# Moving two small SBUF tiles ahead of the split input, so that input and weight blocks lie 256 bytes apart modulo 512

## The chip, the cores and the metric

The kernel runs on one core of one Trainium2 chip. The metric is the device time of one execution in microseconds (us), given as the median of the timed runs. An engine's row in the profile carries a short name: PE is the tensor engine's matmuls, PEld its loads of the stationary operand (LDWEIGHTS), DVE the vector engine, ACT the scalar engine, POOL and SP the other two. SBUF is the on-chip memory of 128 partitions; an offset in bytes below is always the offset within a partition.

## The reference, cut to what matters

Two layers of a decoder trunk on 256 tokens of 1024 channels, all in float32:

```python
for l in range(DEPTH):                      # 2
    h = _mixer(x, ...)                      # x @ w_in, then three branches:
                                            #   gated linear attention, retention, dilated window attention
                                            #   per-channel sigmoid gates, branch projections, merged @ w_out
    x = _layer_norm(ALPHA * x + h, ...)
    f = (silu(x @ w_gate) * (x @ w_up)) @ w_down
    x = _layer_norm(ALPHA * x + f, ...)
```

Nearly all arithmetic is products of the 256 tokens with weights that are used once.

## The kernel before

**Exact float32 products from float32r parts.** Every operand of a product with weights is split into two parts of type float32r: a rounded part (hi) and the rest (lo). A product then takes three matmuls: hi by hi, hi by lo and lo by hi. The layer's input is held split and transposed in the tiles `xh` (hi) and `xl` (lo), 8192 bytes each per partition (8 k-tiles of 256 tokens). The weights stream from HBM in 342 units of 128x1024 float32 into six `stage` buffers; ACT rounds a unit into one block of the pool `R` and DVE subtracts to make its lo part in another (`make_hi`, `make_lo`, recorded under line 118). `R` has 24 blocks of 4096 bytes, named `r` in the profile; the pools `F4` (7 blocks of 4160 bytes) and `F2` (10 of 2048), both named `f`, hold everything else.

**Two kinds of product.** Both are recorded under line 130, and a row names the output first, then the stationary and the moving operand among its inputs without telling which is which; the width does:

- `a_pair` computes [128 columns, 256 tokens]. The weights, 128 columns of an `r` block, are the stationary operand; 256 tokens of `xh` or `xl` are the moving one. Rows: `pm<-xh,r` and `pm<-xl,r`, 128x256. Used for the queries and keys of the dilated attention, for the merge gates, and for all but 512 channels of the SwiGLU.
- `b_group` computes [128 tokens, 512 columns]. 128 tokens of `xh` or `xl` are stationary and 512 columns of an `r` block move. Rows: `pm<-r,xh` and `pm<-r,xl`, 128x512. For the dilated groups' values the 128 tokens are every second one of 256 (`dl` = 2), so that the stationary operand spans 1024 bytes instead of 512.

Where the other operand is itself an activation that was split into `R` blocks, both operands are `r`: the branch projections (`pm<-r,r`, 128x256) and the SwiGLU's down projection (`px<-r,r`, 128x512). The gate of the linear attention multiplies `xh` and `xl` with the small tiles `gah` and `gal` (16 columns stationary, 64 bytes for each k-tile, 256 tokens moving; rows `px<-xh,gah` and so on).

**Order of the work.** The program's order on every engine is fixed when it is written, by a rough clock of costs that decides when side work (attention, norms, the next unit's split) is put between the products. In each layer the stages follow one another: dilated attention's projections, the other branches' projections, merge gates with branch projections, output projection and norm, SwiGLU in pairs of 128 columns (gate and up for one pair are 96 matmuls of 256 columns, then 24 of 512 for a pair's down projection), norm.

**Where tiles lie.** A pool hands out SBUF in the order in which tiles are first allocated, each rounded up to 32 bytes. Between the first `r` block and `xh` lie 24 x 4096 + 7 x 4160 + 10 x 2048 = 147904 bytes, which is 448 modulo 512; `xl` follows 8192 bytes later. So a slice of `xh` or `xl` that starts at a multiple of 512 bytes in its tile (those of lines 377 to 381 do; the odd tokens lie 4 bytes on) stands 64 bytes *behind* a slice of an `r` block, modulo 512, and two slices of `r` blocks stand 0 apart. After `xl` come the `stage` buffers, the constants, `pcol`, `edec` (32 bytes), `xres`, `gah`, `gal`, `hcol` (256 bytes) and the rest. By their sizes `gah` starts 352 bytes past `xh` modulo 512, `gal` too, and each k-tile of 16 columns in them 64 bytes past the one before.

Of the kernel before, what the change touches and what calls it, by code (L numbers as in the profile page):

```python
# [17 lines left out]
L = 2  # L18
# [4 lines left out]
ALPHA = (2 * L) ** 0.25  # L23
# [31 lines left out]
def trunk(ctx: ExitStack, tc: tile.TileContext, wst, xt_in, x_in, cst, tri, pcol, wga, wa2, lnp, out):  # L55
# [5 lines left out]
    def T(shape, tag, bufs=1, dt=F32):  # L61
        return sb.tile(shape, dt, tag=tag, name=tag, bufs=bufs)

    # ---- a rough clock in ns for each engine and tile: side work goes to the tensor engine when its operands
    # should be there, so that the products with the weights needn't wait behind it ----
    clk = {"P": 0.0, "A": 0.0, "V": 0.0, "G": 0.0, "D": 0.0}
# [7 lines left out]
    def when(log, ap, e):  # L74
        """When the last access in this log to any of the columns is over, as seen by engine e."""
        name, a, b = span(ap)
        return max([t + (e != "P" and OWN if by == e else HOP) for x, y, t, by in log.get(name, ()) if x < b and a < y], default=0.0)
# [44 lines left out]
    A = Timed(nc.scalar, "A", 0.833, 110)  # L122
# [17 lines left out]
    def settle(*aps, margin=MARGIN):  # L140
        """For a side generator: go on when these tiles should be there."""
        while any(when(written, a, "P") + margin > clk["P"] for a in aps):
            yield

# [1 line left out]
    class Blocks:  # L146
# [3 lines left out]
        def get(self, n=1):  # L150
            """For a side generator: the next n free blocks."""
            while len(self.free) < n:
                yield
            return [self.free.pop(0) for _ in range(n)]

        def main(self, n=1):
            """For the main stream."""
            left = 3000
            while len(self.free) < n:
                tick()  # L160
                left -= 1
                assert left, "blocks"
            return [self.free.pop(0) for _ in range(n)]
# [4 lines left out]
    R = Blocks(sb, NR, 1024, "r", F32R)  # L168
    F4 = Blocks(sb, N4, 1040, "f4")
    F2 = Blocks(sb, N2, 512, "f2")  # L170
    PM = Blocks(psp, 3, 512, "pm")
    PS = Blocks(psp, 5, 512, "px")

# [1 line left out]
    state = {"dma": 0, "made": 0, "whole": 0, "calm": False, "touched": 0, "freed": 0, "cap": NR // 2}  # L175
    staged, parts = {}, {}
    total = L * UNITS

    def halves(u):
        """The first unit goes by halves, for an early start."""  # L180
        return (slice(0, 512), slice(512, 1024)) if u == 0 else (slice(0, 1024),)
# [61 lines left out]

# [1 line left out]
    side = []  # L245
# [4 lines left out]
    def tick():  # L250
        for g in list(side):
            try:
                next(g)
            except StopIteration:
                side.remove(g)
        # the next unit: its first part when the engine is free for it, the second when the first should be there
        need = state["touched"] + 2
        late = clk["P"] + (CALM if state["calm"] else BACKLOG)
        if state["whole"] < state["made"]:
            hi = parts[state["whole"]][0]  # L260
            if state["whole"] < need or max(clk["V"], when(written, hi, "V")) < late:
                make_lo()
        if state["made"] < min(total, state["touched"] + AHEAD, state["whole"] + 2) and can_make():
            u = state["made"]
            there = u in staged and when(written, staged[u], "A") < clk["P"] + READY
            if u < need or there and min(clk["A"], clk["V"] - SWITCH) < late:
                make_hi()
# [14 lines left out]

# [1 line left out]
    XH = T([128, KT, S], "xh", 1, F32R)  # L284
    XL = T([128, KT, S], "xl", 1, F32R)
    xts = [F2.main()[0] for _ in range(4)]

    # the input comes in five pieces of k-tiles: 0, 1, 2-3, 4-5, 6-7
    PIECES = ((0, 1), (1, 2), (2, 4), (4, 6), (6, 8))
# [13 lines left out]

    # products of zeros while the first loads are under way bring the tensor engine to its full clock
    zero = F2.main()[0]
# [15 lines left out]
    PC = T([128, L, 32], "pcol")  # L321
    # the turning tables fill 32 partitions of their columns; the gate's second matrix and its bias lie beside them
    WA2 = C[32:49, COLS["dilc"][0]:COLS["dils"][1]].rearrange("p (l c) -> p l c", l=L)
    edec = T([128, 8], "edec")
    scr = {g: dram.tile([S, 520], F32, tag=f"scr{g}", name=f"scr{g}") for g in (1, 2)}
    xres = T([128, 2, D], "xres")
    GH = T([128, L, KT * 16], "gah", 1, F32R)
    GL = T([128, L, KT * 16], "gal", 1, F32R)
    hcol = T([128, L, 32], "hcol")
    TRI = T([128, 256], "tri", 1, F32R)  # L330

    def start_rest():
        """What the first products don't need."""
        dma(nc.scalar, C[0:32, 0:512], cst[0:32, 0:512], 32)
# [30 lines left out]
    half = T([128, 4], "half")  # L365
    V.memset(half, -0.5)
    one = T([128, 1], "one")
# [14 lines left out]

# [1 line left out]
    def tokens(v, tt, dl):  # L384
        """128 tokens: the tt-th half, or with dl = 2 those of remainder tt by 2."""
        return v[:, tt * 128:tt * 128 + 128] if dl == 1 else v.rearrange("p (i c) -> p c i", c=2)[:, tt, :]
# [11 lines left out]
    def b_group(units, lh, ll, tt, ps, dl=1, last=False):  # L398
        """ps [128 tokens, 512] from units of [2 k-tiles, 512 columns], a step for each unit."""
        n = len(units)  # L400
        for i, u in enumerate(units):
            b_unit(u, i, n, lh, ll, tt, ps, dl)
            if last:
                free(u)
            if i < n - 1:
                tick()

    def a_pair(units, rh, rl, ps):
        """ps [128 columns, 2, 256 tokens] from units of [4 k-tiles, 256 columns]."""
        n = len(units)  # L410
# [21 lines left out]

# [1 line left out]
    def ln_first(tt, c, ps, st):  # L434
# [36 lines left out]

# [1 line left out]
    def dil_rot(g, ps, dst):  # L473
        """Two heads' channels [128, 2, 256 tokens] into dst, their first 32 turned; dilated groups have even tokens first."""
        dl = 2 if g else 1
# [15 lines left out]
    def dil_group(l, g, dblk, m, den, outs):  # L491
        """Scores, softmax numerators and their products with v; outs gets [128 tokens, 512] for each tile."""
        qb, kb = dblk[g, 0], dblk[g, 1]
# [117 lines left out]

# [1 line left out]
    def gla_gates(l, E):  # L613
# [147 lines left out]

# [1 line left out]
    def ret_all(l, pss, vb, sg):  # L763
# [102 lines left out]
    def head_out(l, key, o, col):  # L866
        """A branch's [tokens, heads] transposed, times its norm's gain when col is given, and split."""
        OH, OL = OT[l, key] = yield from R.get(2)
# [22 lines left out]

# [1 line left out]
    for l in range(L):  # L893
# [3 lines left out]

        # the projections for the branches: a step by tokens has two tiles, one by channels two pairs of heads
        douts = {}
# [26 lines left out]

        # the first two have their units in turns: either tile of tokens, or piece of the first input, gives them work
        us = take(8)
# [61 lines left out]

        # merge gates and branch projections, by pairs of 128 columns
        state["cap"] = (NR - 10) // 2
# [39 lines left out]

        # output projection, then the first norm
        state["cap"] = (NR - 4) // 2
# [16 lines left out]

        # SwiGLU: the first 512 channels by tokens, the others by channels
        state["cap"] = (NR - 5) // 2
# [91 lines left out]
        for tt in range(2):  # L1145
            # of the last tile, the first half of the columns ends before the second begins
            st = T([128, 2, 6], "lnst", 2)
# [60 lines left out]
def _sums(np):  # L1208
    """Within each chunk of 64, a sixteenth of the sum up to a token and of the sum after it."""
    i = np.arange(128)  # L1210
    r, q = i[:, None], i[None, :]
    same = (r // 64) == (q // 64)
    return np.concatenate([np.where(same & (r <= q), 1 / 16, 0.0), np.where(same & (r > q), 1 / 16, 0.0)], 1).astype(np.float32)


def _stream(np, w_in, w_branch, w_out, w_gate, w_up, w_down):
    """All weights in the order of use, as units of [128, 1024]."""
    w = np.empty((L * UNITS, 128, 1024), np.float32)
# [100 lines left out]
```

## Time and profile before

| | |
|---|---|
| median of 3 timed runs | 1068.72 us (1066.67 to 1068.91) |
| the profiled execution's span, first to last instruction | 1066.5 us |
| PE busy | 1049.8 us (98%), 7122 matmuls |
| PEld busy | 956.9 us (90%) |
| DVE busy | 706.6 us (66%) |
| ACT busy | 491.8 us (46%) |
| DMA | 192.25 MB, mean 180 GB/s |

The page gives no other time of the profiled execution than its span; the lowest timed run lies 0.2 us above it, the median 2.2 us. PE's busy time runs from a matmul's start to its modelled end, so neighbouring matmuls overlap, and neither the busy time nor the mean duration of one says how fast they follow each other. That is read from the start times: the distance between two starts, divided by the number of matmuls that started in between. It is called the pace below.

### The profile page before, as it was taken

The page shows a single profiled execution, that of the slowest core. Times are in us where ns is not written, and L with a number is a line of the kernel's source. Part 1 is how long each engine was busy: PE and PEld are TensorE (multiplying, and loading weights), DVE is VectorE, ACT ScalarE, POOL GpSimd, SP SyncE. Part 2 cuts the span into 40 slices and gives each one's busy share as a digit, 9 for nine tenths or more (in the row PEclk, how much of TensorE's full clock was granted, in tenths as well). Part 3 has the DMA queues.
Part 4 walks back from the last instruction along what each step waited for, and adds up shares of the span by engine and source line. Part 5 has one row for each costly group of instructions (what it writes and reads, how often), then busy time and mean ns, then how long its engine had stood idle before and what let it go on. Part 6 is the DMA issues. An engine that isn't in the chain of part 4 may idle for free.

```text
span 1066.5 us, 17475 instructions
## 1 busy us (share of the span) xinstructions
PE 1049.8 (98%) x7122; PEld 956.9 (90%) x7122; DVE 706.6 (66%) x1065; ACT 491.8 (46%) x734; POOL 17.9 (2%) x24
## 2 busy tenths in 40 slices
PE   9999999999999999999999998999999999999997
PEld 7998977799998899999889998877999988999996
DVE  6798755767658756554688777476676686556454
ACT  6475554444445444343364554553443445444330
POOL 0000000000000000000000000000000000000000
PEclk9999999999999999999999999999999999999999
DMA  8786633426656574555376355343375666655521
GB/s 325 248 267 194 197 109 111 158 80 225 190 172 223 168 287 164 194 191 200 121 268 220 124 173 183 92 136 122 118 220 185 186 209 232 223 197 167 194 94 40
DMA packets 55667, 192.25 MB, mean 180 GB/s; under 512 B 6258, under 2 KB 7410, under 8 KB 55587
## 3 DMA queue, kind: packets, MB, share of 16 engines
q1 hardware_dynamic: 50400, 180.38, 51.4%
q10 hardware_dynamic: 5186, 10.76, 3.0%
q8 instruction: 56, 0.92, 0.3%
q14 instruction: 25, 0.20, 0.1%
HBM read 187.93 MB, written 3.18 MB: 179 GB/s over the span
## 4 chain that ended last, share of the span: by engine, by line
PE 90%; DVE 4%; DMA 3%; ACT 1%; issue 1%; SPq 0%; ACTq 0%; DVEq 0%
PE pm L130 70%; PE px L130 18%; DVE f L118 2%; PE px L134 2%; DMA scr<-f 2%; DVE r L118 2%; ACT f L118 1%; DMA stage<-in_wst_dram 0%; DMA f<-scr 0%; ACT r L118 0%; DVE xres L118 0%; SPq L138 0%; ACTq L138 0%; DVE lnst L118 0%; DVEq L1314 0%
## 5 line engine op out<-in xcount | busy, mean ns | idle before, releaser
L130 PE MATMUL pm<-xh,r 128*128 128x256 f32 x2688 | 478.2, 280 | 0.0
L118 DVE SCALAR_TENSOR_TENSOR r<-stage,r 128x1024 fp32r<-128x1024 f32 (+1 forms) x341 | 401.7, 1213 | 59.4 <-ACT r L118 57.1
L130 PEld LDWEIGHTS pm<-xh,r 128*128 128x128 f32 x2688 | 413.1, 189 | 1.1
L118 ACT ACTIVATE r<-stage 128x1024 fp32r<-128x1024 f32 (+1 forms) x328 | 332.8, 1051 | 91.8 <-issue 31.3
L130 PE MATMUL pm<-xl,r 128*128 128x256 f32 x1344 | 374.9, 279 | 0.0
L130 PEld LDWEIGHTS pm<-xl,r 128*128 128x128 f32 x1344 | 252.4, 188 | 0.9
L130 PE MATMUL pm<-r,xh 128*128 128x512 f32 x672 | 218.4, 406 | 0.8 <-ACT r L118 0.8
L130 PEld LDWEIGHTS pm<-r,xh 128*128 128x128 f32 x672 | 124.8, 192 | 29.3 <-issue 3.0
L130 PE MATMUL pm<-r,xl 128*128 128x512 f32 x336 | 133.6, 398 | 0.0
L118 ACT ACTIVATE f<-pm 128x512 f32<-128x512 f32 x72 | 50.8, 707 | 156.6 <-PE pm L130 106.1
L130 PE MATMUL px<-r,r 128*128 128x512 f32 x528 | 122.6, 389 | 0.0
L130 PEld LDWEIGHTS px<-r,r 128*128 128x128 f32 x528 | 97.9, 188 | 19.3
L130 PE MATMUL pm<-r,r 128*128 128x256 f32 (+1 forms) x768 | 115.1, 310 | 0.0
L130 PEld LDWEIGHTS pm<-r,r 128*128 128x128 f32 x768 | 105.2, 191 | 7.3
L118 DVE SCALAR_TENSOR_TENSOR f<-f,pm 128x512 f32<-128x512 f32 x52 | 35.6, 685 | 106.6 <-ACT f L118 89.9
L130 PEld LDWEIGHTS pm<-r,xl 128*128 128x128 f32 x336 | 64.6, 192 | 14.3
L130 PE MATMUL px<-f,f 128*128 128x128 f32 (+4 forms) x368 | 60.4, 304 | 6.3 <-DVE f L118 6.3
L130 PEld LDWEIGHTS px<-f,f 128*128 128x128 f32 (+2 forms) x368 | 48.7, 185 | 16.7 <-issue 8.5
L118 ACT ACTIVATE r<-f 128x512 fp32r<-128x512 f32 x28 | 17.7, 632 | 98.9 <-DVE f L118 98.9
L118 ACT ACTIVATE f<-pm,hcol 128x256 f32<-128x256 f32 x48 | 20.1, 471 | 58.1 <-PE pm L130 58.1
L118 ACT ACTIVATE f<-px 128x512 f32<-128x512 f32 (+2 forms) x52 | 25.0, 507 | 42.6 <-PE px L130 29.4
L118 DVE TENSOR_TENSOR f<-f,pm 128x512 f32<-128x512 f32 x22 | 15.1, 687 | 41.0 <-PE pm L130 40.8
(102 smaller groups left out, 498.6 us busy)
## 6 DMA issues: line engine op xcount, KB each, us to landing
stage<-in_wst_dram SPq DMA_DIRECT2D x339, 512.0 KB, 4.5
f<-in_lnp_dram ACTq DMA_DIRECT2D x8, 512.0 KB, 6.3
scr<-f ACTq DMA_DIRECT2D x8, 260.0 KB, 4.8
f<-scr ACTq DMA_DIRECT2D x4, 520.0 KB, 3.6
xres<-in_x_dram ACTq DMA_DIRECT2D x4, 256.0 KB, 4.0
out_dram<-xres SPq DMA_DIRECT2D x4, 256.0 KB, 2.0
f<-in_xt_dram SPq DMA_DIRECT2D x3, 256.0 KB, 9.1
cst<-in_cst_dram ACTq DMA_DIRECT2D x4, 192.0 KB, 3.8
```

The lines of the kernel that those rows point to most:

```text
L118: return f(*a, **k)
L130: return nc.tensor.matmul(out, lhsT, rhs, **k)
L134: return nc.tensor.transpose(out, in_, ident)
```

## The change

`hcol` and `edec` are allocated ahead of `xh`, with an unused tile of 32 bytes (`gap`) behind them: 256 + 32 + 32 = 320 bytes. The two later allocations go. Comments and documentation strings are emptied too. No instruction is added, removed or moved: the order of all instructions on all engines is the same.

```diff
+    hcol = T([128, L, 32], "hcol")
+    edec = T([128, 8], "edec")
+    T([128, 8], "gap")
     XH = T([128, KT, S], "xh", 1, F32R)
     XL = T([128, KT, S], "xl", 1, F32R)
     xts = [F2.main()[0] for _ in range(4)]
...
     WA2 = C[32:49, COLS["dilc"][0]:COLS["dils"][1]].rearrange("p (l c) -> p l c", l=L)
-    edec = T([128, 8], "edec")
     scr = {g: dram.tile([S, 520], F32, tag=f"scr{g}", name=f"scr{g}") for g in (1, 2)}
     xres = T([128, 2, D], "xres")
     GH = T([128, L, KT * 16], "gah", 1, F32R)
     GL = T([128, L, KT * 16], "gal", 1, F32R)
-    hcol = T([128, L, 32], "hcol")
     TRI = T([128, 256], "tri", 1, F32R)
```

So the distance from the first `r` block to `xh` becomes 147904 + 320 = 148224 bytes, 256 modulo 512. The `stage` buffers and the constants move by the same 320 bytes, `xres`, `gah` and `gal` by 288, what follows by 32. The pools `R`, `F4` and `F2` stay where they are.

## Rows read from the trace of the kernel before

**Rows 1.** The page's first part: busy us, share of the span, instructions.

```profile
span 1066.5 us, 17475 instructions
PE 1049.8 (98%) x7122; PEld 956.9 (90%) x7122; DVE 706.6 (66%) x1065; ACT 491.8 (46%) x734; POOL 17.9 (2%) x24
```

**Rows 2.** Windows: us, busy and count by engine, granted clock, DMA share, GB/s.

```profile
450.00:500.00 50.00, 50.00 (x360) 47.19 (x360) 26.64 (x27) 20.51 (x25) 0.00 (x0) 1.00 0.57 190
...
650.00:700.00 50.00, 46.83 (x273) 39.79 (x272) 27.86 (x50) 25.35 (x47) 1.05 (x2) 0.97 0.41 125
```

**Rows 3.** The chain that ended last: start us, us, what ran.

```profile
77.44 3.45 DVE r L118 x3
...
393.50 11.31 PE pm L130 x96
404.80 5.44 PE px L130 x24
```

**Rows 4.** Groups of PE instructions, shapes apart: count, busy us, mean ns, idle.

```profile
L130 PE MATMUL pm<-xh,r 128*128 128x256 f32 x2688 | 478.2, 280 | 0.0
L130 PE MATMUL pm<-xl,r 128*128 128x256 f32 x1344 | 374.9, 279 | 0.0
L130 PE MATMUL pm<-r,xh 128*128 128x512 f32 x672 | 218.4, 406 | 0.8 <-ACT r L118 0.8
L130 PE MATMUL pm<-r,xl 128*128 128x512 f32 x336 | 133.6, 398 | 0.0
...
L130 PE MATMUL pm<-r,r 128*128 128x256 f32 x576 | 70.9, 283 | 0.0
```

**Rows 5.** Timeline of PE in the first layer's dilated projections: start us, us.

```profile
30.49 0.28 PE L130 MATMUL pm<-xh,r 128*128 128x256 f32 x1
...
52.27 0.63 PE L130 MATMUL pm<-r,xh 128*128 128x512 f32 x2
...
119.09 0.28 PE L130 MATMUL pm<-xl,r 128*128 128x256 f32 x1
...
131.46 0.28 PE L130 MATMUL pm<-xl,r 128*128 128x256 f32 x1
```

**Rows 6.** Timeline of PE in the merge gates: branch projection, then gates, then branch.

```profile
266.51 8.78 PE L130 MATMUL pm<-r,r 128*128 128x256 f32 x72
275.13 0.29 PE L130 MATMUL pm<-xh,r 128*128 128x256 f32 x1
...
291.47 1.70 PE L130 MATMUL pm<-r,r 128*128 128x256 f32 x13
```

**Rows 7.** Timeline of PE, products of 512 columns: every second token, then all.

```profile
55.08 0.62 PE L130 MATMUL pm<-r,xh 128*128 128x512 f32 x2
...
59.98 0.63 PE L130 MATMUL pm<-r,xh 128*128 128x512 f32 x2
...
149.66 0.62 PE L130 MATMUL pm<-r,xh 128*128 128x512 f32 x2
...
155.15 0.62 PE L130 MATMUL pm<-r,xh 128*128 128x512 f32 x2
```

**Rows 8.** Timeline of PE, first layer's products with the small gate matrix.

```profile
133.67 0.28 PE L130 MATMUL px<-xh,gal 128*16 128x256 f32 x1
...
134.03 0.28 PE L130 MATMUL px<-xh,gal 128*16 128x256 f32 x1
...
135.43 0.28 PE L130 MATMUL px<-xh,gal 128*16 128x256 f32 x1
...
135.77 0.28 PE L130 MATMUL px<-xh,gal 128*16 128x256 f32 x1
```

**Rows 9.** Groups of DVE instructions: count, busy us, mean ns, idle before.

```profile
L118 DVE SCALAR_TENSOR_TENSOR r<-stage,r 128x1024 fp32r<-128x1024 f32 x339 | 400.3, 1216 | 57.4 <-ACT r L118 55.2 <-DVE r L118 0.5
```

## The prediction

> **What bounds the kernel now.** I read the page's head first: PE is busy 98% of a span of 1066.5 us, DVE, the next, 66% [rows 1]. The windows then say where that holds. In the SwiGLU PE has no idle time at all while DVE is busy for 26.6 of 50 us and the clock is granted in full, its level of 2.4 GHz; the worst window, around the second layer's dilated attention, has 3.2 us of idle PE in 50 [rows 2]. The chain of work that ended last runs through PE for 90% of its length; the SwiGLU pieces in it follow each other without a gap, 96 matmuls in 11.31 us and 24 in 5.44, while in the dilated stage it passes to DVE for a few us at a time [rows 3]. So almost everywhere the time is the number of matmuls times the pace at which they follow each other, and the pace is all that a change of addresses can touch on PE.
>
> The paces are not the same for the same shape. With weights from `r` stationary and 256 tokens of `xh` or `xl` moving, I find two and only two steady ones:
>
> - 113.4 ns: 192 matmuls from 30.49 to 52.27 us [rows 5], and 144 from 275.13 to 291.47, 113.5 ns with the changeover [rows 6];
> - 117.8 ns: 105 matmuls from 119.09 to 131.46 us [rows 5], and each SwiGLU pair, 11.31 us for 96 [rows 3].
>
> A run keeps the pace it has at its start for dozens of matmuls, and whichever `r` blocks and k-tiles come next don't matter. With both operands in `r` and the same 256 columns it is a third: 72 in 8.62 us, 119.7 ns, right between two runs at the faster pace [rows 6]. Same engine, shape, type and clock; what differs is the distance between the addresses that are read at once, 0 modulo 512 there and 64 bytes here. While a matmul streams, the next one's weights are loaded, so both reads go on together. With 512 moving columns of `r` and tokens stationary the pace is 228.8 ns (24 matmuls from 149.66 to 155.15), and 233.3 ns where every second token is taken (21 from 55.08 to 59.98) [rows 7]; with both in `r`, distance 0, it is 226.7 [rows 3]. Distance matters there too, but 0 is not the bad case.
>
> **What the change does, part by part.** No instruction is moved, so nothing queues differently; only distances change. `xh` and `xl` against `r` go from 64 bytes behind to 256 away, both as moving and as stationary operand.
>
> *256-column products with xh or xl*, 2688 + 1344 = 4032 of them [rows 4]. I counted where the slower pace stands. In the SwiGLU, 8 of 9 pairs of each layer have it: 2 x 8 x 96 = 1536 matmuls, the pieces like the one in [rows 3]. In the dilated projections it is 11 of 24 steps of 48, 528 matmuls, such as the second stretch of [rows 5]. In the first quarter of the merge gates it is some 225 of 288. Together about 2290; the other 1740 are already at 113.4. If all go at the faster pace, the gain is 2290 x 4.4 ns = 10.1 us. If all settle at 117.8, the loss is 1740 x 4.4 = 7.7 us; if all go as the `r` by `r` ones at 119.7, it is 2290 x 1.9 + 1740 x 6.3 = 15.3 us.
>
> Which? No steady run of this shape stands at a distance of 256. The nearest rows are those of the small gate matrix: 16 columns stationary, whose start moves by 64 bytes with each k-tile, so that one stretch of 24 matmuls samples the distances. By the tile sizes, while the weights of k-tile 2 are loaded the stream starts 32 bytes past them (160 - 2 x 64), and those three matmuls take 0.36 us, 120 ns each; with k-tile 7 it starts 224 bytes past (160 - 7 x 64 + 512), and they take 0.34, 113.3 each [rows 8]. The second layer repeats both. In between the paces lie in between, and not evenly: 288 bytes, k-tile 6, gives about 115.7. So near 0 is the worst of them and near 256 the best, and I take 113.4 for all 4032. The weak point is that a load of 16 columns reads an eighth of what a full one does.
>
> The Trainium skill speaks against any effect. Its page "SBUF — State Buffer", section "Who interferes with whom", gives the tensor engine two independent read ports, one for the moving operand and one for LDWEIGHTS, and says that only the port pair shared by VectorE and GpSimd causes contention. By that rule the distance is worth nothing and the change would be worth 0 instead of 10.1 us. The trace doesn't agree: 119.7 beside 113.5 ns within 25 us [rows 6].
>
> *512-column products with xh or xl stationary*, 672 + 336 in `pm` [rows 4]. Some 800 run at about 229, some 180 at 233.3. Down to 226.7 they would give 800 x 2.3 = 1.8 us and 180 x 6.6 = 1.2; up to 233.3 the first kind would lose 3.6. I take the 1.8 and nothing for every second token, because that stationary read spans 1024 bytes and meets all distances whatever its start.
>
> *The rest of PE.* The 576 `r` by `r` products of 256 columns [rows 4] and the down projections keep their distance: 0. The 48 products with `gah` and `gal` still run through eight starts 64 bytes apart: at most 48 x 7 ns, 0.3 us, either way; I take 0.
>
> *DVE, ACT and DMA.* `stage` and `xres` move as well. The 339 splits of a unit take 1216 ns each [rows 9]. The cover is DVE's idle third and PE's full queue; without it, 1% on every split would be 4 us. I take 0.
>
> *What is given back.* Where the chain passes through DVE [rows 3], a faster PE only waits longer: four of the slow dilated steps of the first layer lie around such pieces, 4 x 48 x 4.4 ns = 0.8 us, and I allow 0.2 more for the second layer: 1.0 us.
>
> Sum: -10.1 - 1.8 + 1.0 = -10.9 us, a span of 1055.6. The median lies 2.2 us above the profiled span, so 1057.8 us.
>
> **Rivals.**
>
> 1. *Partial.* At 256 some runs still lock into a slower pace, as two exist now at one distance; the 288-byte sample at 115.7 speaks for it. A mean pace of 114.5 gives 4032 x 1.4 ns = 5.6 us less than today's 115.9 (2290 at 117.8 and 1740 at 113.4), with half of the second term and of what is given back about 1063.
> 2. *Slower.* The moving stream reads 1024 bytes in about the time in which the load reads 512, so it passes over every residue twice and must meet the load somewhere, whatever the distance at the start; 64 behind may be a lucky one, with a state in which the meeting falls between two loads, and 256 puts it in the middle of each. The two paces at one distance speak for it, the gate samples against. At 117.8 for all the time is 1068.7 + 7.7 = 1076.4; at 119.7, 1084. It decides from a mean pace of 115.9 upwards.
> 3. *No change.* Paces come from how a run starts and not from the distance: 1068.7. For it: the same distance has both. Against it: the paces of 119.7 and 113.5 in turns in [rows 6], and the samples in [rows 8]. This is how it would go by the rule on the tensor engine's two ports in the Trainium skill's page "SBUF — State Buffer".
>
> That the tiles don't land as said is not a rival: the distance of 256 follows from the sizes.
>
> **How the numbers follow.** My forecast has 0.45, the partial gain 0.21, no change 0.13, slower 0.21. The predicted time is the forecast's, 1057.8. About 0.2%, 2 us, is what a measurement tells from no change; by the cases faster has 0.66, same 0.13, slower 0.21. Below, the forecast with the 1.2 us of the second-token products and nothing given back comes to 1055.6; a pace under 113.4, which no row excludes, would need 0.9 ns for another 3.6 us, so 1052. Above, I go to the first price of the slower rival, 1076. Outside remain the 119.7 case and a floor that falls much further, under 2 in 10. The forecast's own range is 1054 to 1061.
>
> **What would show it.** Right: the SwiGLU pieces of the chain fall from 11.31 to 10.88 us for 96, the gates stay at 113.5, the products with all tokens stationary come to 226.7, the `r` by `r` ones stay at 119.7 and 226.7, and PE's idle time grows by about 1 us in the dilated windows. Wrong: SwiGLU pieces at 11.31 or 11.5 us, gates above 113.5, or the faster pace everywhere and the end no earlier, with the waits on DVE grown by as much.

## The result and the profile after

The change made the kernel slower: 1083.49 us (1080.97 to 1084.82, 4 runs) against 1068.82 (1066.67 to 1069.72, 4 runs), a ratio of 1.0136 [1.0117, 1.0155]. I had forecast 1057.8.

The head of the page after, busy us and share by engine:

```profile
span 1082.8 us, 17475 instructions
PE 1064.7 (98%) x7122; PEld 972.7 (90%) x7122; DVE 706.9 (65%) x1065; ACT 491.7 (45%) x734; POOL 17.9 (2%) x24
```

Instructions, DVE and ACT are those of [rows 1]. The span grew by 16.3 us: PE's busy time by 14.9 and its idle time by 1.4 (1082.8 - 1064.7 = 18.1 against 16.7).

A window of after, in its SwiGLU, columns as in [rows 2]:

```profile
450.00:500.00 50.00, 50.00 (x358) 47.28 (x357) 25.70 (x28) 19.82 (x24) 0.00 (x0) 1.00 0.55 190
```

The clock is granted in full in the SwiGLU as before, and PE has no idle time there; it gets through 358 matmuls where it had 360. So PE is slower at an unchanged clock and with nothing to wait for.

The chain that ended last, of after; start us, us, what ran:

```profile
246.60 101.31 PE pm L130 x780
...
389.34 10.91 PE px L130 x48
400.25 11.51 PE pm L130 x96
411.76 5.47 PE px L130 x24
```

A SwiGLU pair takes 11.51 us for 96, 119.9 ns each, where [rows 3] have 11.31; the 24 down products are at 5.47 against 5.44. The piece of gates and branches, 780 matmuls, is 101.31 us; in the chain of before it is 98.42:

```profile
243.14 98.42 PE pm L130 x780
```

Timeline of PE after, at the places of [rows 5 and 6]:

```profile
30.33 0.28 PE L130 MATMUL pm<-xh,r 128*128 128x256 f32 x1
...
53.36 0.63 PE L130 MATMUL pm<-r,xh 128*128 128x512 f32 x2
...
253.64 0.28 PE L130 MATMUL pm<-xh,r 128*128 128x256 f32 x1
...
270.92 1.36 PE L130 MATMUL pm<-r,r 128*128 128x256 f32 x10
...
279.56 0.28 PE L130 MATMUL pm<-xh,r 128*128 128x256 f32 x1
```

From 30.33 to 53.36 us 192 matmuls follow each other at 119.9 ns, where they had 113.4; from 253.64 to 270.92 it is 144 gate products at 120.0, where [rows 6] have 113.5; and from 270.92 to 279.56 the 72 `r` by `r` ones at 120.0, as before. Both operand pairs, once 6 ns apart, have one pace now, and every long stretch of `xh` or `xl` against `r` in the kernel settles at 120.0 ns, whatever it comes out of. There is no second pace any more.

Timeline of PE after for the 512-column products, as in [rows 7], and for the small gate matrix, as in [rows 8]:

```profile
55.45 0.63 PE L130 MATMUL pm<-r,xh 128*128 128x512 f32 x2
...
60.35 0.63 PE L130 MATMUL pm<-r,xh 128*128 128x512 f32 x2
...
134.93 0.28 PE L130 MATMUL px<-xh,gal 128*16 128x256 f32 x1
...
135.28 0.28 PE L130 MATMUL px<-xh,gal 128*16 128x256 f32 x1
...
135.63 0.28 PE L130 MATMUL px<-xh,gal 128*16 128x256 f32 x1
...
135.97 0.28 PE L130 MATMUL px<-xh,gal 128*16 128x256 f32 x1
...
154.15 0.62 PE L130 MATMUL pm<-r,xh 128*128 128x512 f32 x2
...
158.23 0.62 PE L130 MATMUL pm<-r,xh 128*128 128x512 f32 x2
```

All tokens stationary: 18 matmuls from 154.15 to 158.23 us, 226.7 ns each. Every second token: 21 from 55.45 to 60.35, 233.3 as before. The gate matrix's stretch passes other starts than before. Counted as in [rows 8], by the weights that are loaded meanwhile, the stream starts 128 bytes past them from 134.93 us (k-tile 1, 116.7 ns a matmul) and 0 bytes past from 135.63 (k-tile 3, 113.3).

DVE's splits, the group of [rows 9], kept their time:

```profile
L118 DVE SCALAR_TENSOR_TENSOR r<-stage,r 128x1024 fp32r<-128x1024 f32 x339 | 400.4, 1216 | 62.2 <-ACT r L118 60.0 <-DVE r L118 0.5
```

### The profile page after: what moved, and what is told of

It reads as the page before. It is cut to its first block, busy times and chain, and to the rows that moved or that the text cites. A ratio compares the mean times of both kernels' runs of the same rounds, so it can differ in the third digit from the quotient of the medians.

```text
span 1082.8 us, 17475 instructions
## 1 busy us (share of the span) xinstructions
PE 1064.7 (98%) x7122; PEld 972.7 (90%) x7122; DVE 706.9 (65%) x1065; ACT 491.7 (45%) x734; POOL 17.9 (2%) x24
## 4 chain that ended last, share of the span: by engine, by line
PE 93%; DMA 3%; DVE 2%; ACT 1%; issue 1%; SPq 0%; ACTq 0%; DVEq 0%
PE pm L130 73%; PE px L130 18%; PE px L134 2%; DMA scr<-f 2%; DVE f L118 1%; DVE r L118 1%; ACT f L118 1%; DMA f<-scr 1%; DMA stage<-in_wst_dram 0%; ACT r L118 0%; DVE xres L118 0%; SPq L138 0%; ACTq L138 0%; DVE lnst L118 0%; DVEq L1316 0%
## 5 line engine op out<-in xcount | busy, mean ns | idle before, releaser
L130 PE MATMUL pm<-xh,r 128*128 128x256 f32 x2688 | 494.1, 284 | 0.0
L130 PEld LDWEIGHTS pm<-xh,r 128*128 128x128 f32 x2688 | 422.6, 192 | 1.2
L130 PE MATMUL pm<-xl,r 128*128 128x256 f32 x1344 | 380.2, 283 | 0.0
L130 PEld LDWEIGHTS pm<-xl,r 128*128 128x128 f32 x1344 | 257.8, 192 | 0.9
```

The lines of the kernel that those rows point to most:

```text
L130: return nc.tensor.matmul(out, lhsT, rhs, **k)
```

## The experiments

Below, "distance" is the address of `xh` less that of an `r` block, modulo 512: 448 in the kernel before, 256 in the changed one. Paces of the SwiGLU are a pair's piece of the chain over its 96.

**Place or distance.** The change moved `stage`, `xres` and `xh` as well as their distance. Here the small tiles go ahead of the pool `R` instead: the moved tiles lie where the change puts them, but `r` (with `F4` and `F2`) moves along, so that the distance is 448 again.

```diff
+    hcol = T([128, L, 32], "hcol")
+    edec = T([128, 8], "edec")
+    T([128, 8], "gap")
     R = Blocks(sb, NR, 1024, "r", F32R)
```

> The two small tiles and the gap stand ahead of the R blocks instead of ahead of xh. xh, stage, xres and all that follows keep the addresses of the changed kernel, but R moves with them, so the distance of xh from R is again 64 bytes behind. If the distance sets the pace (theory 'distance'): two paces of 113.4 and 117.8 ns as before, a span of about 1066.5 us. If the place of xh or of what moved with it sets it (theory 'place'): 120.0 ns everywhere and 1083 us.

1069.16 us (8 runs) against 1068.74, ratio 1.0002 [0.9988, 1.0016]. Its chain:

```profile
243.69 98.42 PE pm L130 x780
...
394.43 11.31 PE pm L130 x96
```

Pairs are at 117.8 ns as in [rows 3]. It's the distance.

**Other distances, and the period.** These take the kernel before and put a gap ahead of `xh`, whose width sets the distance (16 columns of 4 bytes, as shown, for 0; 48 for 128; 64 for 192):

```diff
+    T([128, 16], "gap")
     XH = T([128, KT, S], "xh", 1, F32R)
```

Distance 0: 

> Kernel before with a gap of 64 bytes ahead of xh: distance 0. The products of two R blocks ran at 120 ns at this distance, so 'distance' expects 120.0 ns for all 4032 products of 256 columns and 226.7 for those of 512 (every second token apart): 4032 x 6.6 - 10.4 = 16 us more in the first, 2.4 less in the second, about 1080 us. 'place' expects no rule: anything from 1060 to 1083.

Distance 128: 

> Kernel before with a gap of 192 bytes: distance 128. If paces repeat every 256 bytes ('period 256', since 0 and 256 both gave 120.0), 128 is half a period away from both and should be the clean one: 113.4 ns for all, about 1056 us. If they repeat every 512 only ('period 512'), 128 is nothing special: between 113.4 and 120, about 1066 to 1083 us.

Distance 192: 

> Kernel before with a gap of 256 bytes: distance 192, which is the old 448 less 256. 'period 256': the old picture again, runs at 113.4 and at 117.8 ns, about 1066.5 us. 'period 512', with 256 as the worst point: 119 to 120 ns, about 1080 us.

Measured 1087.44, 1081.69 and 1067.21 us (one run each) beside 1068.74 for the kernel before. The chains, at 0:

```profile
249.27 101.31 PE pm L130 x780
...
402.94 11.51 PE pm L130 x96
```

at 128:

```profile
246.49 100.72 PE pm L130 x780
...
399.95 11.52 PE pm L130 x96
```

and at 192:

```profile
242.65 98.42 PE pm L130 x780
...
393.00 11.31 PE pm L130 x96
```

Distance 0 repeats both pieces of distance 256 to the last digit, and 192 both of 448. (The span at 0 is 2.9 us longer than at 256; 2.7 of it lie ahead of the longer piece, which starts at 249.27 us and not at 246.60. Of these, 1.5 arise before the first stretch of `xh` against `r`: near the start, twelve products of 512 columns follow each other at 427 ns, where the changed kernel has five.) So in both pairs tried the paces repeat after 256 bytes. Half way between, 128 isn't the clean one, with pairs at 120.0 ns. The change moved `xh` from 64 bytes short of a multiple of 256 onto one, and that is as bad as 0.

**Is there a better one between?** Distance 224 is the change with the smallest tile, the gap of 32 bytes, left out; the others are gaps of 56, 32 and 24 columns in the kernel before; 96, a gap of 40, was run later.

Distance 224: 

> The changed kernel without its 32-byte gap tile: distance 224, that is 32 short of 256. Theory 'smooth' (the nearer to 0 modulo 256, the nearer to 120 ns): between 192 (113.4 and 117.8 ns) and 256 (120), about 118 to 120, 1074 to 1083 us. Theory 'grain' (only the 64-byte line in which each read starts counts): like 192 or like 256, 1067 or 1083. Theory 'sweet spot' (the slower paces come from the stream catching up with the load, and 192 stands just beside the distance at which it doesn't): 113.4 ns throughout, about 1056.

Distance 160: 

> Distance 160, between 128 (118.7 and 120.0 ns) and 192. 'smooth': about 117 ns, 1070 to 1075 us. 'grain': like 128, 1081, or like 192, 1067. 'sweet spot', if it lies on this side: 113.4 ns, about 1056.

Distance 64: 

> Distance 64, the mirror of 192 modulo 256. If only the size of the distance counted, it would show the paces of 192 and 1067 us. If the sign counts (the stream is ahead of the load here, behind it there), it may be anything between 113.4 and 120 ns, 1056 to 1083 us.

Distance 32: 

> Distance 32. 'grain' and 'smooth': like 0, 120 ns, 1083 us. 'sweet spot' on this side of 0: 113.4 ns, about 1056 us.

Distance 96: 

> The last multiple of 32 bytes modulo 256 that has not been run, distance 96, between 64 (117.7 ns, 1081.1 us) and 128 (119.3 ns, 1081.7 us). If the pace goes evenly between neighbours, 118.5 ns and about 1081 us. If each 32 bytes has a pace of its own, as 160 and 224 had, anything from 113.4 ns (1057 us) to 120 (1085 us), and not 118.5.

224 took 1080.19 us (4 runs; 1.0128 [1.0101, 1.0154]), 160 took 1083.99 (4 runs; 1.0164 [1.0142, 1.0185]), both against 1066.88; 64 took 1081.08 and 32 took 1075.25, one run each beside the same; 96 took 1089.84, one run beside 1068.14, the slowest of all. Their chains, at 32:

```profile
245.21 100.35 PE pm L130 x780
...
398.15 11.20 PE pm L130 x96
```

64:

```profile
246.38 100.36 PE pm L130 x780
...
399.46 11.31 PE pm L130 x96
```

96:

```profile
248.26 101.29 PE pm L130 x780
...
402.56 11.52 PE pm L130 x96
```

160:

```profile
247.44 100.31 PE pm L130 x780
...
400.55 11.39 PE pm L130 x96
```

and 224:

```profile
243.84 100.55 PE pm L130 x780
...
397.13 11.36 PE pm L130 x96
```

From 0 to 224 a pair's pace goes 119.9, 116.7, 117.8, 120.0, 120.0, 118.6, 117.8, 118.3 ns: the pace jumps from one step of 32 bytes to another, so neither "smooth" nor "grain" of 64 bytes holds, no distance is the "sweet spot" with 113.4 throughout, and none tried is clearly better than 448. At 32 the pairs are faster than before (11.20) and the gates slower (100.35): it has two paces as well, since 144 gates there take 16.97 us, 117.8 ns each.

```profile
252.24 0.28 PE L130 MATMUL pm<-xh,r 128*128 128x256 f32 x1
...
269.21 1.00 PE L130 MATMUL pm<-r,r 128*128 128x256 f32 x7
```

The traces of 64, 128 and 160 show two as well, those of 0, 96, 224 and 256 only one. The even guess for 96 (118.5 ns) was wrong too; there the 512-column products are slow as well. Only at 192 and 448 do the gates reach 113.4.

**What decides between the two paces at 448.** Runs of 113.4 and of 117.8 come from the same addresses, so something other than the distance chooses. These put matmuls ahead of each SwiGLU pair from 1 to 8 of the kernel before, into the bank that the pair then overwrites, so that the output doesn't change (`touch` gives the hi and lo blocks of a unit of weights; the order of all other matmuls stays):

```diff
             pg = PM.main()[0]
+            if p:
+                hi, _ = touch(ug[0])
+                mm(pg[:, 256:512], hi[:, 0:128], hi[:, 256:512], start=True, stop=True)
             a_pair(ug, xh, xl, pg)
```

One `r` by `r`, as shown: 

> The kernel before, with one matmul more ahead of each of the SwiGLU's pairs 1 to 8: two weight blocks of r with each other, 128 by 256, into the half of the bank that the pair overwrites. The results do not change. Theory 'entry': at the distance of before the products just ahead decide between 113.4 and 117.8 ns; the pairs come out of down projections (both operands in r, 512 columns) and stay at 117.8, the merge gates come out of r by r products of 256 columns and stay at 113.4. Then the pairs go at 113.4: 16 x 96 x 4.4 ns = 6.7 us less, 16 x 0.12 = 1.9 us more, about 1064 us, faster than both kernels. Rival 'stage': the SwiGLU has its pace for another reason (which blocks of r, which load on the side): pairs stay at 117.8 and the time is 1068.7 + 1.9 = 1070.6 us.

Four of them: 

> The same with four such matmuls ahead of each pair, in case that one is too few to change what the pair enters from. 'Entry': pairs at 113.4 ns, 16 x 4 x 0.12 = 7.7 us more and 6.7 less, about 1069.7 us. 'Stage': pairs at 117.8, 1076.4 us. If the pairs change here and not with one, the entry takes several products to settle.

One with `xh` stationary and 512 columns of `r`, `mm(pg, xh(0)[:, 0:128], hi[:, 0:512], ...)`: 

> The same with one matmul of another kind ahead of each pair: 128 tokens of xh stationary, 512 columns of r moving, as in the projections after which the first layer's SwiGLU pair 0 runs at 113.4 ns. 'Entry': pairs at 113.4, 16 x 0.23 = 3.7 us more and 6.7 less, about 1065.7 us. 'Stage': pairs at 117.8, 1072.4 us.

One `r` by `r` left the pairs where they were: 1071.85 us against 1068.14, 1.0025 [1.0012, 1.0038] (12 runs). Its chain, pairs 1 and then 7 with 8:

```profile
393.20 11.42 PE pm L130 x97
...
494.64 22.85 PE pm L130 x194
```

Four made pairs 1 to 7 fast, (11.37 - 0.48) / 96 = 113.4 ns, but cost more than they gave (64 x 0.12 us against 14 x 0.42): 1072.26 us (one run).

```profile
394.34 11.37 PE pm L130 x100
```

One with `xh` stationary did it too, and is faster than the kernel before: 1065.60 us, 0.9977 [0.9966, 0.9989] (12 runs).

```profile
392.96 11.13 PE pm L130 x97
...
492.48 22.67 PE pm L130 x194
```

11.13 less the added 0.23 us is 10.90, 113.5 ns. But pairs 7 and 8 together take 22.67: less 10.90 and two added products, 11.31, so pair 8 is at 117.8. It follows pair 7 with only the added matmul between, and that one threw it back. So the same product ahead can turn a slow stretch fast and a fast one slow. The next runs leave it out ahead of pair 8 (`if 0 < p < NPAIR - 1`), and shorten it.

512 columns: 

> The kernel before with the one matmul of 128 tokens of xh by 512 columns of r ahead of pairs 1 to 7 only. Pair 8 follows pair 7 with no down projection between; with the matmul ahead of it too it fell back from 113.4 to 117.8 ns. If a stretch keeps its pace until something else comes between ('entry'), pair 8 now stays at 113.4: 2 x (96 x 4.4 + 228) ns = 1.3 us less than with pair 8's, about 1064.3 us. If pair 8 is slow for a reason of its own, 117.8 stays there and the time is 1065.2 us.

256 columns: 

> The same with 256 columns of r moving in that matmul instead of 512. It costs 14 x 0.115 = 1.6 us instead of 3.2. If it's the operands that set the entry, the pairs go at 113.4 ns, about 1062.7 us; if its length counts, they may stay at 117.8, about 1070.3 us.

128 columns: 

> The same with 128 columns, a product shorter than the load of the next weights (0.19 us in the rows). Costs 14 x about 0.1 = 1.4 us at most. With the operands deciding, the pairs at 113.4 ns and about 1062.5 us; with the length deciding, 117.8 and about 1070 us, or another pace.

1065.77 us, 0.9965 [0.9948, 0.9982] (12 runs); 1063.88 us, 0.9953 [0.9941, 0.9966] (5 runs); and 1063.61 (one run), beside 1069.60. The chain with 512 columns, pair 1 and then 7 with 8:

```profile
395.93 11.13 PE pm L130 x97
...
495.45 22.01 PE pm L130 x193
```

and with 256:

```profile
394.38 11.01 PE pm L130 x97
...
493.18 21.89 PE pm L130 x193
```

Pair 8 now stays fast (22.01 less 0.23 is 21.78 for 192, 113.4 ns): a stretch keeps its pace until something comes between. With 256 columns (11.01 - 0.12) / 96 is 113.4 ns again, and with 128 a pair's piece is 11.01 too: that one added product with `xh` stationary was enough here, at all three lengths. It also differs from the `r` by `r` one in the part of the bank that it writes and in the columns that move, and no run tells these apart. The version with 256 columns beats both kernels, by 0.47% the one before.

But the products ahead don't settle it alone. Up to the SwiGLU the version with 512 columns is the kernel before, and yet its first stretch of 192 went at (52.48 - 29.87) / 192 = 117.8 ns in the profiled execution, where [rows 5] have 113.4:

```profile
29.87 0.28 PE L130 MATMUL pm<-xh,r 128*128 128x256 f32 x1
...
52.48 0.40 PE L130 MATMUL pm<-r,xh 128*128 128x512 f32 x1
```

That is 0.8 of the 1.5 us by which this version missed its expected time. What else chooses, the moment at which a stretch begins or another thing, was not tested.

## Why the prediction was wrong

**What bounds the kernel** held. PE is 98% busy after, the SwiGLU's time is matmuls times pace, and the whole loss but 1.4 us is PE's busy time.

**That the distance sets the pace** held as well: the first experiment left the tiles at their new places and had the old time. The Trainium skill's rule, in "SBUF — State Buffer", section "Who interferes with whom", that the tensor engine's two read ports are independent, would have given no change; here a distance is worth 14.7 us, and 21.7 at 96.

**The step that failed** is "near 0 is the worst of them and near 256 the best, and I take 113.4 for all 4032". At 256 the pace is 120.0 ns, the one that the `r` by `r` products had in [rows 6] at 0, and distance 0 gives the same. I took the price from the loads of 16 columns in [rows 8], and they don't rank the distances. In the run with the small tiles ahead of `R`, k-tile 3 has distance 0 in both layers (the second layer's weights lie 512 bytes on); it takes 113.3 ns a matmul in the first and 116.7 in the second:

```profile
134.28 0.28 PE L130 MATMUL px<-xh,gal 128*16 128x256 f32 x1
...
134.62 0.28 PE L130 MATMUL px<-xh,gal 128*16 128x256 f32 x1
...
659.70 0.28 PE L130 MATMUL px<-xh,gal 128*16 128x256 f32 x1
...
660.05 0.28 PE L130 MATMUL px<-xh,gal 128*16 128x256 f32 x1
```

Nor do they agree with full loads, which have 120 at 0 and, in the SwiGLU, 116.7 at 32 and 118.3 at 224, where [rows 8] gave 120 and 113.3. So two samples of three matmuls, each read once a layer, were taken for a rule; the weak point that I named, the size of the load, is only a part of it. The nearest row by shape was the third pace in [rows 6], a full load at a multiple of 256, and I had its price beside it: "if all go as the `r` by `r` ones at 119.7, it is 2290 x 1.9 + 1740 x 6.3 = 15.3 us", 1084. With the 120.0 that the runs show it is 2290 x 2.2 + 1740 x 6.6 = 16.5; summed from start to start in the two traces, the 4032 products took 16.0 us more (485.9 against 469.9). I gave the slower rival, of which this was the dearer case, 0.21, and put it outside the range.

Of that rival's mechanism, a stream that meets each load somewhere, the runs bear out that 448 has a good place that 256 lacks; they don't show where in a load the reads meet. That 64 behind is "a lucky one" holds among the distances tried, though 192 is as lucky.

**The 512-column products with all tokens stationary** came to 226.7 ns as said. That is a gain where the 256-column ones lose, at the same distance. Its size was off: some 800 products gave back about 1.0 us by their pace and not 1.8, since many stretches start with five to ten slower ones before they settle. (Longer steps, where these stretches begin, break off or wait, differ by another 0.9.) Every second token stationary stayed at 233.3: 0, as taken.

**The rest of PE, DVE and DMA.** The `r` by `r` products of 256 columns kept about 120 ns, DVE's splits 1216 ns. The down projections, which I had at 0, start each group of 24 a little slower now (5.47 us against 5.44), about 0.4 us in all. `gah` and `gal` stayed within 0.1 us.

**What is given back** rested on a faster PE that waits longer for DVE. PE became slower, and its idle time still rose, by 1.4 us, the rest of the loss. Most of that is `px` products that wait for DVE (us in total, times, longest), before:

```profile
PE px L130 <- DVE f L118: 7.7, 4, 3.2
```

and after:

```profile
PE px L130 <- DVE f L118: 8.9, 3, 3.8
```

So this wait doesn't go simply by how fast PE is.

**Partial and no change** fell: not one steady stretch at 256 is under 119.9 ns. What I listed for them, two paces at one distance, is real at 448 and 192, and at 32, 64, 128 and 160 too, but 256 has only one.

Open is what in the chip repeats after 256 bytes, why 512-column products like the distances 0 and 256 that 256-column ones like least, why the same product ahead turns a slow stretch fast and a fast one slow, and why an untouched stretch changed its pace. Nothing here looks inside a load.

## What to carry to other kernels

Where PE is busy all the time and one shape shows several paces at a full clock, the distance between the addresses of the stationary and the moving operand, modulo 256 bytes here, is worth up to 2% of the time, and it has to be measured with the very shape that carries the time, in long stretches: another width ranks the distances otherwise, and a few short loads gave no rank at all. If one distance has two paces, look at what runs just ahead of a slow stretch: one cheap product with other operands, 0.12 us, moved a stretch of 96 by 0.42 us, and it should be left out where the stretch is fast already. Watch the stretches that no edit touches as well: one of them changed its pace here. Price the bad case by the nearest full-size row that you have, and let the range hold it.

## What the runs showed of the hardware that I had not expected

- With 128 by 128 stationary and 256 float32r columns moving, the pace goes with the distance of the two operands and repeated after 256 bytes (0 and 256: 119.9 ns a product in the SwiGLU; 192 and 448: 117.8 there and 113.4 in the gates); the steps of 32 bytes between give 116.7 to 120.0 there, in no even order.
- With 512 columns of `r` moving and tokens stationary the order is another: 226.7 ns at 0 and 256, where 448 has 228.8 [rows 7]; but 96, as slow as 256 for 256 columns, has about 234 here too.
- At distance 448 there are two steady paces, 113.4 and 117.8 ns. A stretch keeps its own for as long as nothing comes between (192 products, the longest here), and a single product with `xh` stationary ahead of it, 0.06 to 0.23 us long, can change which.
